# A gated convolution and pooling trunk: the input projection in pairs of blocks by seven partial products, its weight sums on GpSimd, its gates parked in DRAM

## The chip, the core and the metric

The kernel runs on one core of a Trainium2 chip. The metric is the device time of one execution in microseconds (us), here the median of several runs. A core has TensorE (PE, matrix products into the PSUM memory, whose weight loads are listed as PEld), VectorE (DVE), ScalarE (ACT), GpSimd (POOL) and SyncE (SP), which mostly issues DMAs. The engines run side by side, each through its own queue in a fixed order, and wait for one another by semaphores. SBUF is the on-chip memory that all engines and the DMAs reach.

## The reference

1024 prompt tokens with 16 meta tokens ahead of them, and 64 sample tokens (8 sequences of 8), pass one layer in float32; D is 1024.

```python
h = rmsnorm(x, norm_g)
z = einsum('btd,de->bte', h, w_in)          # w_in is 1024 x 7168
a_val, a_gate, a_silu, p_in, p_silu, g_a, g_b = split(z, 7)
u = a_val * sigmoid(a_gate)
c = causal_depthwise_conv(u, conv_w, conv_b) # width 31, per channel
c = silu(layernorm(c)) * silu(a_silu)
br_a = c @ w_conv_out
pooled = trailing_mean(p_in, 2/4/8/16 by channel group) - p_in
q = (pooled @ w_pool_mix, per group) * pool_scale * silu(p_silu)
br_b = q @ w_pool_out
y = x + (sigmoid(g_a) * br_a + sigmoid(g_b) * br_b) @ w_out
return rmsnorm(y, final_g), last 30 rows of u, last 15 rows of p_in
```

## The kernel before

Channels lie on the 128 partitions and tokens along the columns (1104 columns, 1088 without the meta tokens). Each matrix product is made of three float32r products: an operand is cut into a high part h (a rounded copy, ACT, `split` L98) and a low part l (the value minus h, DVE, L99), and `gemm` (L119 to L132, the matmul at L129) adds wh·xh + wh·xl + wl·xh in PSUM.

One block is 128 columns of w_in. It takes 8 slices of channels × 3 passes × 3 pieces of columns = 72 matmuls of 362 to 368 columns, each with its own weight load. w_in has 56 such blocks: convolution value and gate (`pv`, `pg` in `glu`), SiLU path (`psl`), pool input (`pp`), pool gate (`pps`), merge gates (`pga`, `pgb`). `load_w` fetches a block's 512 KB and splits it on ACT and DVE, three blocks ahead.

Order of the work: the first five `pp` blocks (NX = 5) multiply x·g before the RMS factor is known; the factor `rms` comes from `root_stats` and `spread`; then DVE scales x (L272) and it is split into hh and hl. Then come the pooling groups (`pool_in` with its window sums at L304 to L309, `pool_gates`, `pool_mix`). Then `ORDER` interleaves `glu`, `branch_b` (gate block `pgb` and projection `ppo`), `gate_a` and `silu_path`. A `glu` step ends with a convolution chunk (`conv_chunk`): 31 taps, one on ACT and 30 on DVE as scalar_tensor_tensor c = e·w + c (L378 for the prompt, L379 for the sample), put later in the order by CONV_LATER. Then LayerNorm (`pmean`, L462, `vsum`), `branch_a` (L475 to L477 and a split), the merge (`pco`, L500) and the output projection (`pwo`, L549). The engine queues' order comes from a list scheduler by program order and priority; two stretches at the start are fixed by hand.

GpSimd does little: memsets, and the copy of the sample's state into the extended tiles (L289, 120 columns; L404, 240 columns). SBUF work tiles come from 38 slots; PSUM has two tiles of three banks and two of one bank.

Of the kernel before, what the change touches and what calls it, by code (L numbers as in the profile page):

```python
# [10 lines left out]
ALU = mybir.AluOpType  # L11

P = 128
D = 1024
NK = D // P
META = 16
# [7 lines left out]
TP2 = SEQ  # L24
# [3 lines left out]
# Columns of a PSUM tile's three banks: of all tokens, and of all but the meta tokens. Counts are even.  # L28
CUT1 = (0, N1, 2 * N1, TALL)
CUT2 = (0, 364, 726, T2)  # L30
EW = CB + TP + DB * (CB + DS)
PW = TP + DB * (PB + DS)
# [3 lines left out]
NSLOT = 38  # L36
CONV_LATER = 4000
WARM = 8
NX = 5
# [10 lines left out]
def hybrid_trunk_kernel(  # L50
# [25 lines left out]
    wp = ctx.enter_context(tc.tile_pool(name="wp", bufs=3))  # L76
# [3 lines left out]
    ps3 = ctx.enter_context(tc.tile_pool(name="ps3", bufs=2, space=bass.MemoryType.PSUM))  # L80
    ps1 = ctx.enter_context(tc.tile_pool(name="ps1", bufs=2, space=bass.MemoryType.PSUM))

    def slot(name, n=T2, dt=F32):
        return sl.tile([P, n], dt, tag="slot", name=name, bufs=NSLOT, padded_shape=[P, TALL])

    def bank3(name):
        return ps3.tile([P, 3, 512], F32, tag="bank3", name=name)
# [9 lines left out]
    def split(dst_h, dst_l, src):  # L97
        act.copy(dst_h, src)  # L98
        dve.tensor_tensor(dst_l, src, dst_h.bitcast(F32), ALU.subtract)  # L99

    def load_w(src, name):
        raw = wp.tile([P, NK, P], F32, tag="raw", name=f"raw_{name}", bufs=2)
        h = wp.tile([P, NK, P], F32R, tag="wh", name=f"wh_{name}")
        l = wp.tile([P, NK, P], F32R, tag="wl", name=f"wl_{name}")
        sp.dma_start(out=raw, in_=src)

        def ready():
            split(h, l, raw)
# [13 lines left out]

    def gemm(out, w, xs, c0, cut, ns=range(3), nk=NK, m0=0, ks=None):
        wh, wl = w
        xh, xl = xs
        for k in ks or range(nk):
            for i, (a, b) in enumerate(((wh, xh), (wh, xl), (wl, xh))):
                for j in ns:
                    pe.matmul(  # L129
                        out[:, j, : cut[j + 1] - cut[j]],  # L130
                        a[:, k, m0 : m0 + P],
                        b[k][:, c0 + cut[j] : c0 + cut[j + 1]],  # L132
                        start=(k == 0 and i == 0),
                        stop=(k == nk - 1 and i == 2),
                    )
# [4 lines left out]
    # The pieces of a PSUM tile cut by CUT2, each with its columns of an SBUF tile.  # L140
    def pieces(ps, t):
        n, m = CUT2[1], CUT2[2] - CUT2[1]
        return (ps[:, 0, :n], t[:, :n]), (ps[:, 1:, :m], v3(t[:, n:], m))
# [9 lines left out]
    # 1 / sqrt(mean + eps) with tokens on partitions, a tile of tokens per pair of columns, from the  # L153
    # squares summed over chunks.
    def root_stats(ssum, n, eps, name):
        tiles = token_tiles(n)
        nt = len(tiles)
        ps = ps1.tile([P, 512], F32, tag="ps1", name=f"pst_{name}")
# [9 lines left out]
    # The factors of root_stats with tokens along the columns, on every partition.  # L168
    def spread(r, n, name):
        tiles = token_tiles(n)  # L170
        nt = len(tiles)
        out = slot(f"ir_{name}", n)
        for g in range(0, nt, 4):
            ps = ps1.tile([P, 512], F32, tag="ps1", name=f"pb_{name}{g}")
            part = tiles[g : g + 4]
            dg = slot(f"dg_{name}{g}", 4 * P)
# [12 lines left out]
    # The first NX blocks multiply x * g, and take the token's factor after the product.  # L189
    xs = [slot(f"x{k}", TALL) for k in range(NK)]  # L190
    xg = tuple([slot(f"xg{s}{k}", TALL, F32R) for k in range(NK)] for s in "hl")
# [13 lines left out]
    # Products that nothing reads bring the tensor engine to its full clock while the first loads run.  # L205
    warm = ps1.tile([P, 512], F32, tag="ps1", name="warm")
    for _ in range(WARM):
        pe.matmul(warm[:, :P], ones, ones, start=True, stop=True)
    xsum = slot("xsum", TALL)
    w_raw = [wp.tile([P, NK, P], F32, tag="raw", name=f"raw_p{i}", bufs=2) for i in range(2)]  # L210
    w_first = [tuple(wp.tile([P, NK, P], F32R, tag=f"w{s}", name=f"w{s}_p{i}") for s in "hl") for i in range(2)]
# [10 lines left out]
    load_w2 = load_w(w_in[PG + 2], "p2")  # L222
    out_first = [bank3(f"pp{j}") for j in range(2)]
    raws = []

    def keep_raw(j, ps):
        raw = slot(f"rawp{j}", TALL)
        act.copy(v3(raw, N1), ps[:, :, :N1])
        raws.append(raw)

    with tc.manual_schedule(engines={act.engine, dve.engine}):
# [8 lines left out]
        w = load_w2()  # L240
        for k in range(NK):
            for i in range(2):
                gemm(out_first[i], w_first[i], xg, 0, CUT1, ns=(0,), ks=(k,))
        for j in (1, 2):
            for i in range(2):
                gemm(out_first[i], w_first[i], xg, 0, CUT1, ns=(j,))
        act.activation(xsum, xs[0], AF.Square)
        for k in range(1, NK):
            sq = slot(f"xsq{k}", TALL)
# [7 lines left out]
    with tc.manual_schedule(engines={pe.engine}):  # L257
        for j in range(2, NX):
            if j > 2:
                w = load_w_now(w_in[PG + j], f"p{j}")  # L260
            out_raw[j] = bank3(f"pp{j}")
            for k in range(NK):
# [4 lines left out]
                gemm(out_raw[j], w, xg, 0, CUT1, ks=(k,))  # L267
            if j < NX - 1:
                keep_raw(j, out_raw[j])
    hx = ([], [])  # L270
    for k in range(NK):
        dve.scalar_tensor_tensor(xs[k], xs[k], col(OFF_NG, k), rms, ALU.mult, ALU.mult)  # L272
        h, l = slot(f"hh{k}", TALL, F32R), slot(f"hl{k}", TALL, F32R)
        split(h, l, xs[k])
        hx[0].append(h)
        hx[1].append(l)
    keep_raw(NX - 1, out_raw[NX - 1])

# [1 line left out]
    q = ([], [])  # L280
    st = ctx.enter_context(ExitStack())
    stp = st.enter_context(tc.tile_pool(name="stp", bufs=2))

    def pool_in(j, ps, pooled):
        e = stp.tile([P, PW], F32, tag="pe", name=f"pe{j}")
        es = e[:, TP:].rearrange("p (b t) -> p b t", t=PB + DS)
        stg = stp.tile([P, DB, PB], F32, tag="pst", name=f"pst{j}")
        sp.dma_start(out=stg, in_=spool[j])
        pool.tensor_copy(es[:, :, :PB], stg)  # L289
        if j < NX:  # L290
            dve.tensor_tensor(e[:, :TP], raws[j][:, :TP], rms[:, :TP], ALU.mult)
            dve.tensor_tensor(es[:, :, PB:], v3(raws[j][:, TP:], DS), v3(rms[:, TP:], DS), ALU.mult)
        else:
            act.copy(v3(e[:, : 2 * N1], N1), ps[:, :2, :N1])
            act.copy(e[:, 2 * N1 : TP], ps[:, 2, : TP - 2 * N1])
            act.copy(es[:, :, PB:], v3(ps[:, 2, TP - 2 * N1 : N1], DS))
# [369 lines left out]
```

## Time and profile before

| | us |
|---|---|
| median of 3 runs | 1015.0 (1014.75 to 1017.23) |
| span of the profiled execution | 1011.5 |
| PE busy | 1000.9 (99%), 5838 matmuls |
| DVE busy | 716.7 (71%) |
| ACT busy | 261.1 (26%) |
| POOL busy | 13.4 (1%) |

The span runs from the first to the last instruction of one profiled execution; a run's time has about 3.5 us around it (1015.0 less 1011.5). Rows of groups give the busy time of all instructions of a kind and the mean duration of one; pipelined instructions overlap, so busy time divided by the count is the spacing, and the mean is longer. Rows of the chain of waits give start, length and engine of each piece of the work that ended last. Rows of the timeline give start, duration, engine, line, operation and operands; x3 at the end of a row merges three.

### The profile page before, as it was taken

What the parts mean: (1) busy time and instruction counts of PE and PEld (TensorE: products, weight loads), DVE (VectorE), ACT (ScalarE), POOL (GpSimd) and SP (SyncE); (2) the same over time, 40 slices, a digit from 0 to 9 for tenths busy, and PEclk for the clock granted to TensorE, in tenths of its full rate; (3) what the DMA queues carried; (4) which work ended last, traced back from release to release, by engine and by line L of the source; (5) the groups of instructions that cost most, each with busy time, mean ns of one, the idle gap of its engine ahead of it and who ended that gap; (6) DMA issues with size and microseconds to landing.
All of it is one profiled execution on the core that took longest, in us unless ns stands there. A gap on an engine that the chain in (4) does not pass through costs nothing.

```text
span 1011.5 us, 13769 instructions
## 1 busy us (share of the span) xinstructions
PE 1000.9 (99%) x5838; PEld 978.2 (97%) x5838; DVE 716.7 (71%) x918; ACT 261.1 (26%) x344; POOL 13.4 (1%) x29
## 2 busy tenths in 40 slices
PE   8999999999999999999999999999999999999997
PEld 7999999999999999999999999999999999997885
DVE  6697753544999959769689799999846934445343
ACT  7644232222211111111121111111245722114111
POOL 0001100000000000000000000000000000000000
PEclk9999999999999999999999999999999999999999
DMA  8222222231212222221221232322111033334322
GB/s 276 68 38 63 61 49 49 45 68 39 48 65 52 90 51 83 69 48 64 70 48 64 68 93 49 101 45 90 64 42 43 23 149 131 130 131 174 124 77 84
DMA packets 45374, 79.02 MB, mean 78 GB/s; under 512 B 22912, under 2 KB 28032, under 8 KB 45312
## 3 DMA queue, kind: packets, MB, share of 16 engines
q1 hardware_dynamic: 43008, 69.22, 23.8%
q10 hardware_dynamic: 2304, 8.91, 2.6%
q8 instruction: 46, 0.75, 0.3%
q14 instruction: 16, 0.13, 0.0%
HBM read 63.09 MB, written 15.03 MB: 77 GB/s over the span
## 4 chain that ended last, share of the span: by engine, by line
PE 96%; DMA 1%; DVE 1%; SPq 0%; issue 0%; ACT 0%; DVEq 0%
PE pg L129 10%; PE pv L129 10%; PE psl L129 9%; PE ppo L129 9%; PE pps L129 9%; PE pga L129 9%; PE pgb L129 9%; PE pco L129 9%; PE pp L129 9%; PE pwo L549 7%; PE pmix L129 2%; DMA raw_wo<-in_w_out 1%; PE pwos L549 1%; DMA raw_p<-in_w_in 1%; DVE wol L99 0%
## 5 line engine op out<-in xcount | busy, mean ns | idle before, releaser
L378 DVE SCALAR_TENSOR_TENSOR c<-ce,pv,c 128x1024 f32<-128x1024 f32 x240 | 307.6, 1283 | 3.1
L379 DVE SCALAR_TENSOR_TENSOR c<-ce,pv,c 128x64 f32<-128x64 f32 x240 | 68.0, 283 | 5.6 <-ACT c L376 1.5
L500 DVE TENSOR_TENSOR lga<-pco,lga 128x364 f32<-128x364 f32 (+1 forms) x16 | 10.8, 719 | 46.8 <-PE pco L129 46.8
L129 PE MATMUL pg<-hh,wh_g 128*128 128x368 f32 x192 | 42.7, 330 | 0.0
L129 PE MATMUL pv<-hh,wh_v 128*128 128x368 f32 x192 | 42.6, 330 | 0.0
L129 PE MATMUL psl<-hh,wl_s 128*128 128x362 f32 (+1 forms) x192 | 42.6, 329 | 0.0
L129 PE MATMUL pg<-hl,wh_g 128*128 128x368 f32 x192 | 42.6, 330 | 0.0
L129 PE MATMUL psl<-hh,wh_s 128*128 128x362 f32 (+1 forms) x192 | 42.6, 329 | 0.0
L129 PE MATMUL pg<-hh,wl_g 128*128 128x368 f32 x192 | 42.6, 330 | 0.0
L129 PE MATMUL pv<-hh,wl_v 128*128 128x368 f32 x192 | 42.5, 330 | 0.0
L129 PE MATMUL pv<-hl,wh_v 128*128 128x368 f32 x192 | 42.5, 329 | 0.0
L129 PE MATMUL ppo<-ql,wh_po 128*128 128x362 f32 (+1 forms) x192 | 42.4, 329 | 0.0
L129 PE MATMUL pps<-hh,wl_ps 128*128 128x362 f32 (+1 forms) x192 | 42.4, 329 | 0.0
L129 PE MATMUL pga<-hh,wl_ga 128*128 128x362 f32 (+1 forms) x192 | 42.4, 329 | 0.0
L129 PE MATMUL pgb<-hh,wl_gb 128*128 128x362 f32 (+1 forms) x192 | 42.3, 328 | 0.0
L129 PE MATMUL ppo<-qh,wl_po 128*128 128x362 f32 (+1 forms) x192 | 42.3, 329 | 0.0
L129 PE MATMUL pco<-cxh,wh_co 128*128 128x362 f32 (+1 forms) x192 | 42.3, 328 | 0.0
L129 PE MATMUL pps<-hl,wh_ps 128*128 128x362 f32 (+1 forms) x192 | 42.2, 328 | 0.0
L129 PE MATMUL pgb<-hl,wh_gb 128*128 128x362 f32 (+1 forms) x192 | 42.2, 328 | 0.0
L129 PE MATMUL pga<-hl,wh_ga 128*128 128x362 f32 (+1 forms) x192 | 42.2, 328 | 0.0
L129 PE MATMUL psl<-hl,wh_s 128*128 128x362 f32 (+1 forms) x192 | 42.2, 328 | 0.0
L129 PE MATMUL pco<-cxl,wh_co 128*128 128x362 f32 (+1 forms) x192 | 42.2, 328 | 0.0
(212 smaller groups left out, 2210.9 us busy)
## 6 DMA issues: line engine op xcount, KB each, us to landing
x<-in_xT SPq DMA_DIRECT2D x24, 184.0 KB, 4.0
d_tb<-gbo ACTq DMA_DIRECT2D x8, 544.0 KB, 2.8
d_sga<-gao ACTq DMA_DIRECT2D x8, 544.0 KB, 3.4
t<-d_tb SPq DMA_DIRECT2D x8, 544.0 KB, 4.5
lga<-d_sga SPq DMA_DIRECT2D x8, 544.0 KB, 5.6
raw_ps<-in_w_in SPq DMA_DIRECT2D x8, 512.0 KB, 3.5
raw_g<-in_w_in SPq DMA_DIRECT2D x8, 512.0 KB, 4.2
raw_v<-in_w_in SPq DMA_DIRECT2D x8, 512.0 KB, 3.5
```

The costliest lines, as they stand in the source:

```text
L129: pe.matmul(out[:, j, : cut[j + 1] - cut[j]], a[:, k, m0 : m0 + P], b[k][:, c0 + cut[j] : c0 + cut[j + 1]], start=(k == 0 and i == 0), sto ...
L378: dve.scalar_tensor_tensor(cp, sp_, wk, cp, ALU.mult, ALU.add)
L379: dve.scalar_tensor_tensor(cs, ss_, wk, cs, ALU.mult, ALU.add)
L500: dve.tensor_tensor(c, p, c, ALU.mult)
L549: pe.matmul(ps[:, n - ns[0], :], x(k), w[k][:, n * 512 : (n + 1) * 512], start=(k == 0 and s == 0), stop=(k == NK - 1 and s == len(passes) ...
```

## The change

Four blocks (NX = 4) stay as they were. The other 52 blocks of w_in are made in 26 pairs by `seven`: a pair's weights are a 2×2 matrix of halves (two blocks × two halves of the 8 channel slices), the input is a 2×2 matrix too (two halves of the channel slices × two halves of the tokens, so the tokens are put in another order on the host), and seven products of half size with sums of their operands take the place of eight. Each product is 2 pieces of 276 (or 272) columns × 4 slices × 3 passes = 24 matmuls; a pair is 168.

- Input operands: seven sets of four tiles (`t_ops`, 28 of the now 37 slots), built once from the scaled x: 16 sums on DVE, 28 splits, of whose low parts 16 are on GpSimd and 12 on DVE.
- Weights, for each pair (`w_sums`): four sums and seven low parts on GpSimd, 11 tensor_tensor of 128×512; the high parts on ACT. Operand tiles: 6 (`wop`).
- Results: ACT copies three intermediate results of each pair out of PSUM (`keep`, 6 copies), DVE adds the others to them (`put`, 8 adds of 272 or 276 columns, PSUM + SBUF).
- PSUM is cut into 8 single banks, of which a pair uses all.
- Convolution: the prompt's taps stay on DVE; the sample's taps become products of 248 columns on GpSimd (8 for a chunk) and a tensor_reduce on DVE (2). `csum`, `vsum`, the sample's window sums and the low parts of pooled, mix weights and q go to GpSimd.
- All gates, the pooled inputs and the convolution results are written to DRAM and fetched again; `pool_mix`, `branch_b` and LayerNorm come after all 26 pairs.

```diff
-ORDER = "c0 b0 c1 b1 b2 c2 b3 b4 c3 b5 b6 c4 b7 a0 c5 a1 a2 c6 a3 a4 c7 a5 a6 a7 s0 s1 s2"
+ORDER = "g0 p2 p3 q0 g1 q1 q2 q3 b0 g2 b1 b2 b3 a0 g3 a1 a2 a3 s0 s1 s2 s3"
...
+    lo_, hi_ = slice(0, HT), slice(HT, TALL)
+    t_ops = {}
+    for name, k0 in (("11", 0), ("21", NQ)):
+        t_ops[name] = x_op(name)
+        for k in range(NQ):
+            x_split(t_ops[name][k], xs[k0 + k][:, lo_], pool if k % 2 else dve)
...
+    for k in range(NQ):
+        t = slot(f"ta{k}", (2, HT))
+        tmp.append(t)
+        dve.tensor_tensor(t[:, 0], xs[k][:, hi_], xs[k][:, lo_], ALU.subtract)
+        dve.tensor_tensor(t[:, 1], xs[NQ + k][:, hi_], t[:, 0], ALU.subtract)
+        x_split(t_ops["T2"][k], t[:, 1], pool if k % 2 else dve)
...
+    def w_sums(src, name):
+        a1, a2 = raw_tile(src[0], f"{name}0"), raw_tile(src[1], f"{name}1")
+        a11, a12, a21, a22 = a1[:, :NQ], a1[:, NQ:], a2[:, :NQ], a2[:, NQ:]
...
+        pool.tensor_tensor(s1, a21, a22, ALU.add)
+        pool.tensor_tensor(s2, s1, a11, ALU.subtract)
+        pool.tensor_tensor(s3, a11, a21, ALU.subtract)
+        pool.tensor_tensor(s4, a12, s2, ALU.subtract)
+        for i, a in enumerate((a11, a12, s2, s3, s1, s4, a22)):
+            o = op_tile(f"wo{i}_{name}", (2, NQ, P))
+            split(o[:, 0], o[:, 1], a, pool)
+            yield o
...
+        def keep(outs, what):
...
+                act.copy(c[:, :w], out[:, :w])
...
+        def put(block, half, outs, cs):
...
+                dve.tensor_tensor(z[block][:, half, cols[u]], out[:, :w], cs[u], ALU.add)
...
+        x = pair("px")
+        product(x, next(ws), t_ops["11"], units, True, False)
+        c1 = keep(x, "c1")
+        y = pair("py")
+        product(y, next(ws), t_ops["21"], units, True, True)
+        put(0, 0, y, c1)
+        product(x, next(ws), t_ops["T2"], units, False, False)
+        c2 = keep(x, "c2")
+        v = pair("pv")
+        product(v, next(ws), t_ops["T3"], units, True, False)
+        product(x, next(ws), t_ops["T1"], units, False, True)
+        c4 = keep(x, "c4")
+        put(1, 1, v, c4)
+        w = pair("pw")
+        product(w, next(ws), t_ops["22"], units, True, True)
+        put(0, 1, w, c4)
+        product(v, next(ws), t_ops["T4"], units, False, True)
+        put(1, 0, v, c2)
+        return z
...
+    def conv_chunk(i, e, es):
...
+                dve.scalar_tensor_tensor(cp, sp_, wk[:, k : k + 1], cp, ALU.mult, ALU.add)
...
+                pool.tensor_tensor(tap[:, b], win, wk.unsqueeze(1).to_broadcast([P, DS, CW]), ALU.mult)
+            dve.tensor_reduce(cs[:, h], tap.rearrange("p b t k -> p (b t) k"), AX.X, ALU.add)
...
+            pool.tensor_tensor(csum[0], csum[0], c, ALU.add)
+        act.dma_start(out=d_c[i], in_=c)
...
+            h, l = halves(fetch(d_pool[j], f"lp{j}"), f"pool{j}", pool)
...
+            h, l = halves(gate, f"q{j}", pool)
...
+            pool.tensor_tensor(vsum, vsum, sq, ALU.add)
```

## Rows read from the trace of the kernel before

**Rows 1.** The page: busy time of the engines, and the chain's shares by engine.

```profile
PE 1000.9 (99%) x5838; PEld 978.2 (97%) x5838; DVE 716.7 (71%) x918; ACT 261.1 (26%) x344; POOL 13.4 (1%) x29
PE 96%; DMA 1%; DVE 1%; SPq 0%; issue 0%; ACT 0%; DVEq 0%
```

**Rows 2.** Chain in order of time: start us, length us, what; whole blocks of the projection.

```profile
47.98 25.84 PE pp L129 x153
...
97.73 6.11 PE pmix L129 x36
103.85 23.91 PE pps L129 x144
...
229.78 12.10 PE pg L129 x72
241.89 12.07 PE pv L129 x72
...
959.51 44.58 PE pwo L549 x192
```

**Rows 3.** Groups of PE by form: operands, columns, count | busy us, mean ns.

```profile
L180 PE MATMUL pb_c<-dg_c,ones 128*128 128x128 f32 x18 | 2.3, 275 | 0.0
L160 PE MATMUL pst_x<-ones,xsum 128*128 128x2 f32 x18 | 2.1, 246 | 0.0
```

**Rows 4.** Timeline of GpSimd: its copies of 120 and 240 columns; start us, duration us.

```profile
25.82 0.52 POOL L289 COPY pe<-pst 128x120 f32<-128x120 f32 x2 [24.88 <-DMA pst<-in_spool]
81.86 1.30 POOL L289 COPY pe<-pst 128x120 f32<-128x120 f32 x1 [55.53 <-DVE pool L309]
...
139.97 0.29 POOL L289 COPY pe<-pst 128x120 f32<-128x120 f32 x1 [24.82 <-DVE pool L309]
...
302.03 0.39 POOL L404 COPY ce<-cst 128x240 f32<-128x240 f32 x1
...
632.63 2.39 POOL L404 COPY ce<-cst 128x240 f32<-128x240 f32 x1
```

**Rows 5.** Timeline of DVE around three of these copies (81.8, 302 and 632 us).

```profile
81.78 1.24 DVE L291 TENSOR_TENSOR pe<-rawp,ir_x 128x1040 f32<-128x1040 f32 x1
...
82.94 1.37 DVE L99 TENSOR_TENSOR pooll<-pool,poolh 128x1088 fp32r<-128x1088 f32 x1
...
302.09 0.93 DVE L405 TENSOR_TENSOR ce<-pv,sg 128x736 f32<-128x736 f32 x1
...
629.90 3.67 DVE L378 SCALAR_TENSOR_TENSOR c<-ce,pv,c 128x1024 f32<-128x1024 f32 x3
633.49 1.29 DVE L388 TENSOR_TENSOR csum<-csum,c 128x1088 f32<-128x1088 f32 x1
634.69 1.41 DVE L378 SCALAR_TENSOR_TENSOR c<-ce,pv,c 128x1024 f32<-128x1024 f32 x1
```

**Rows 6.** Groups of DVE by form: operands, columns, count | busy us, mean ns.

```profile
L378 DVE SCALAR_TENSOR_TENSOR c<-ce,pv,c 128x1024 f32<-128x1024 f32 x240 | 307.6, 1283 | 3.1
L99 DVE TENSOR_TENSOR cxl<-c,cxh 128x1088 fp32r<-128x1088 f32 x8 | 10.1, 1287 | 0.0
L308 DVE SCALAR_TENSOR_TENSOR pool<-pw,pe 128x1024 f32<-128x1024 f32 x8 | 9.8, 1219 | 0.1
L99 DVE TENSOR_TENSOR ml<-mraw,mh 128x512 fp32r<-128x512 f32 x4 | 2.7, 684 | 0.0
L406 DVE TENSOR_TENSOR ce<-pv,sg 128x304 f32<-128x304 f32 x8 | 3.7, 466 | 0.0
```

**Rows 7.** Groups of ACT by form: operands, columns, count | busy us, mean ns.

```profile
L98 ACT CAST mh<-mraw 128x512 fp32r<-128x512 f32 x4 | 2.5, 621 | 4.7 <-DMA mraw<-in_w_mix 4.6
L295 ACT COPY pe<-pp 128x304 f32<-128x304 f32 x3 | 1.2, 413 | 0.0
L467 ACT ACTIVATE csq<-c 128x1088 f32<-128x1088 f32 x7 | 7.8, 1115 | 4.5 <-DVE c L462 4.2
```

**Rows 8.** Timeline of DVE where the RMS factor is ready and x is scaled.

```profile
48.66 10.32 DVE L272 SCALAR_TENSOR_TENSOR x<-x,pv,ir_x 128x1104 f32<-128x1104 f32 x8 [2.58 <-ACT ir_x L185]
```

More of the change, by code (lines that the diff above doesn't have):

```diff
@@ new lines, in product @@
+    def product(outs, w, t, units, first, last):
+        for out, (lo, hi) in zip(outs, units):
+            for k in range(NQ):
+                for i, (a, b) in enumerate(((0, 0), (0, 1), (1, 0))):
+                    pe.matmul(
+                        out[:, : hi - lo],
+                        w[:, a, k],
+                        t[k][:, b, lo:hi],
+                        start=first and k == 0 and i == 0,
+                        stop=k == NQ - 1 and i == 2,
+                        skip_group_check=True,
+                    )
@@ new lines, in pool_window @@
+            pool.tensor_tensor(ss2[:, :, lo:], ss[:, :, lo:], ss[:, :, lo - d : PS - d], ALU.add)
+            s, ss, d = s2, ss2, 2 * d
+        dst = slot(f"pool{j}", (2, H2))
+        dve.scalar_tensor_tensor(
+            dst[:, :, :HP], v3(s[:, META:], HP), 1.0 / w, v3(e[:, META:], HP), ALU.mult, ALU.subtract
+        )
+        for h in range(2):
+            b = slice(h * DB // 2, (h + 1) * DB // 2)
+            dve.scalar_tensor_tensor(
+                v3(dst[:, h, HP:], DS), ss[:, b, PB:], 1.0 / w, es[:, b, PB:], ALU.mult, ALU.subtract
+            )
@@ new lines, in pool_window, with pool_ext, sample, pool_raw @@
+        act.dma_start(out=d_pool[j], in_=dst)
+    def pool_ext(j):
+        e = slot(f"pe{j}", (TP,))
+        es = st.tile([P, DB, PS], F32, tag="pes", name=f"pes{j}")
+        sp.dma_start(out=es[:, :, :PB], in_=spool[j])
+        return (e, es), (v3(e[:, :META], HM), v3(e[:, META:], HP), es[:, :, PB:])
+    def sample(z):
+        return z.rearrange("p h (b t) -> p (h b) t", t=DS)
+    def pool_raw(j):
+        e, (em, ep, es) = pool_ext(j)
+        f = parts(v3(rms, HT))
+        r = parts(v3(raws[j], HT))
+        dve.tensor_tensor(ep, r[1], f[1], ALU.mult)
+        pool.tensor_tensor(em, r[0], f[0], ALU.mult)
+        for h in range(2):
+            b = slice(h * DB // 2, (h + 1) * DB // 2)
+            pool.tensor_tensor(es[:, b], v3(r[2][:, h], DS), v3(f[2][:, h], DS), ALU.mult)
+        pool_window(j, *e)
@@ new lines, in pool_pair, with gate_pair @@
+    def pool_pair(i):
+        z = seven((w_in[PG + 2 * i], w_in[PG + 2 * i + 1]), f"p{i}", UNITS1, t_ops)
+        for b in range(2):
+            e, (em, ep, es) = pool_ext(2 * i + b)
+            zm, zp, zs = parts(z[b])
+            act.copy(em, zm)
+            act.copy(ep, zp)
+            for h in range(2):
+                act.copy(es[:, h * DB // 2 : (h + 1) * DB // 2], v3(zs[:, h], DS))
+            pool_window(2 * i + b, *e)
+    def gate_pair(i, base, name, func, dst):
+        z = seven((w_in[base + 2 * i], w_in[base + 2 * i + 1]), f"{name}{i}", UNITS2, t_ops)
+        for b in range(2):
+            act.activation(z[b], z[b], func)
+            act.dma_start(out=dst[2 * i + b], in_=z[b])
@@ new lines, in hybrid_trunk_kernel, with fetch @@
+    for j in range(NX):
+        with later():
+            pool_raw(j)
+    steps = {
+        "g": glu_pair,
+        "p": pool_pair,
+        "q": lambda i: gate_pair(i, PSG, "q", AF.Silu, d_gate),
+        "b": lambda i: gate_pair(i, GBG, "b", AF.Sigmoid, d_sgb),
+        "a": lambda i: gate_pair(i, GAG, "a", AF.Sigmoid, d_sga),
+        "s": lambda i: gate_pair(i, SG, "s", AF.Silu, d_sa),
+    }
+    for step in ORDER.split():
+        steps[step[0]](int(step[1]))
+    def fetch(src, name):
+        t = slot(name)
+        sp.dma_start(out=t, in_=src)
+        return t
@@ L467, in hybrid_trunk_kernel @@
             act.activation(sq, conv[i], AF.Square)
[L468 to L470 removed]
+            pool.tensor_tensor(vsum, vsum, sq, ALU.add)
+    for d in range(3, 6):
+        branch_b(d)
     rstd = spread(root_stats(vsum, T2, LN_EPS, "c"), T2, "c")
```

473 lines of the change are left out of this document (227 added, 246 removed).

## The prediction

> **What bounds the kernel now.** I read the page's busy times first, then the chain: PE is busy in 99% of the span and carries 96% of the chain [rows 1]. Then the chain in order of time: whole blocks of 72 matmuls follow one another without a gap [rows 2]. So a microsecond taken from PE is one off the time as long as every other engine keeps pace; DVE has 29% of the span free, ACT 74%, GpSimd 99%. Then what those engines would cost: GpSimd's few copies and what runs on DVE beside them [rows 4, 5], and DVE's and ACT's groups [rows 6, 7].
>
> **PE, the part that gains.** A block of 72 takes 12.10 us at 368 columns (168.0 ns a matmul), two of 362.7 take 23.91 us, and 192 matmuls of 512 columns take 44.58 us (232.2 ns) [rows 2]. From 368 to 512 columns that is 0.446 ns a column, so 276 columns come to 127.0 ns and 272 to 125.2 ns. A pair of 168 is 21.3 or 21.0 us. Of the 26 pairs 10 are made over all tokens (8 in the convolution, 2 of pool inputs) and 16 without meta tokens. Before: 10 × 24.17 + 16 × 23.91 = 624 us; after: 10 × 21.3 + 16 × 21.0 = 550 us. Gain 74 us. Could the loads, now 168 for 144, be the bound? Matmuls of 2 columns, which leave a load bare, are spaced by 2.1 / 18 = 117 ns, those of 128 columns (float32) by 128 ns [rows 3]. At 128 ns the stage is 559 us and the gain 65; I take 74.
>
> The Trainium skill (TensorE: Matmul & The Clock Gate, Back-to-back issue gap) gives N/2.4 + 2.5 ns for one matmul, an estimated 117.5 ns at 276 columns and a stage of some 509 us, a gain of 115. For 368 columns it would give 156 ns where the rows have 168.0, so the measurement decides.
>
> **GpSimd alone.** 11 tensor_tensor of 512 columns for each pair, 286 in all; no row of before has GpSimd doing one. Bounds: its copies take 0.26 to 0.29 us for 120 columns and 0.39 us for 240 where nothing stands in their way [rows 4], so 0.16 us and 0.96 ns a column. With both inputs read at once an op of 512 columns takes 0.65 us, with one after the other 1.14 us. I take 1.14: nearly twice DVE's 0.684 us for the same shape [rows 6], and I know no row that lets GpSimd read two streams at once. The Trainium skill (GPSIMD Engine Reference, Elementwise — side-by-side cycle accounting) has 4497 ns for 2048 columns, an estimated 1.12 us for 512; by it the sum would be the same. Of GpSimd's other work: 64 sample-tap products of 248 columns, 8 sums `csum` of 1088, 20 small window sums. All by the same price: 326 + 41 + 17 + 13 = 397 us in a stage of 550. It fits alone.
>
> **DVE alone.** 240 taps, spaced by (3.67 − 1.28) / 2 = 1.195 us [rows 5], stay: 287 us. 40 more with two SBUF inputs of 1024 to 1040 columns (20 window sums, 8 pool results, 4 scalings, 8 GLU products) at 1.14 us, from the 1219 ns of L308 less overlap [rows 6]: 45. 208 `put` of 272 to 276 columns at 0.44 us, below the 466 ns of 304 columns [rows 6]: 92. 16 reductions of 992 columns at 1.2 us: 19. Together 443 us. It fits alone. ACT has for a pair 7 copies of 0.62, 6 of about 0.39 and 2 activations of 1.1 us [rows 7], 9 of 21 us, and DMA stores; hidden, and so are the new DRAM writes and reads beside PE.
>
> **DVE and GpSimd together, the part that loses.** Rows 4 and 5 show that they don't run side by side. The copy at 81.86 takes 1.30 us in place of 0.27: it ends at 83.16, just behind the DVE op that began at 81.78 and ended at 83.02; the DVE op after that takes 1.37 us where its kind takes 1.29 [rows 5, 6]. Five of the eight copies of 120 columns look like this. The copy of 240 columns at 632.63 takes 2.39 us: it waits out a tap and `csum`, and the next tap takes 1.41 in place of 1.28 us. But at 302.03 the copy takes its 0.39 us beside a DVE op whose one input is in PSUM. So a DVE op with two SBUF inputs and a GpSimd op that reads SBUF take turns, and GpSimd's reading comes back as DVE time, less about 0.1 us: 240 columns are 0.23 us of reading and cost the tap 0.13. The Trainium skill (SBUF — State Buffer, Who interferes with whom) states it for each GpSimd instruction that reads SBUF, against each DVE one with two SBUF inputs: an exclusive lock for the whole instruction. The copies agree (1.30 for 0.27 us); a GpSimd op with two inputs is in no run here.
>
> So the two sums add up. GpSimd's turns: 0.98 us of reading less 0.1 = 0.88 us; 286 of them 252 us, sample taps 64 × 0.38 = 24, `csum` 15, the rest 7: 298 us. DVE's: 287 + 45 = 332 us. The input operands add 28 DVE ops of 552 columns at 0.64 and 16 GpSimd ops at 0.96: 33 us. Together 663 us of turns in a stage that PE could do in 550. Nor are they spread evenly: in about four pairs (the second of g0, before there is a convolution, and the last three, after it) DVE has few taps and the turns fill only 10.8 of 21 us, which leaves 41 us unused. The stage then takes 663 + 41 = 704 us, 154 more than PE needs. How this reaches PE: a pair's operands come from GpSimd, at most six ahead, so PE waits at the heads of the pairs, while the taps are finished at leisure.
>
> Bounds: at 0.65 us a GpSimd op (turn 0.39) the turns and gaps come to about 551 us and PE stays the bound; at 1.14 us with nothing overlapped and lost turns as at 632 us they come to 804.
>
> **Hand-overs.** *Start:* `rms` is ready at 48.66 us and the scaled x 10.3 us later [rows 8]; PE then has one direct block less to cover it. It does 153 matmuls from 47.98 [rows 2], of which the last 72 go, and so needs the first set at about 61.7. That set is ready by then; the later ones contend with GpSimd's 16 splits, inside the 663; without contention 3 us. *Mix:* 144 matmuls are 24 us of PE (6.11 us for 36 [rows 2]); GpSimd has 16 low parts of 1088 columns at 0.16 + 2.09 = 2.25 us and 4 of weights, 40.6 us, and a last chain of an ACT copy (1.1) and a low part, some 4 us: 40.6 − 24 + 4 = 21 us of PE waiting; at one stream 4, at worst 25. *LayerNorm:* branch_a has 8 × 3 DVE ops of 1.2 us [rows 6], 29 us, and behind the factor PE has two `ppo` blocks less some 8 us and the first `pco` block to cover it; with the weight splits in between 8 us, between 0 and 15.
>
> **Sum.** 1015 − 624 + 704 + 21 + 8 = 1124 us, made against the execution with a span of 1011.5 and about 3.5 us around it, which stands at the median. With the bounds: 1015 − 624 + 551 + 4 = 946 to 1015 − 624 + 804 + 40 = 1235.
>
> **Rivals.** *The forecast (slower):* taking turns holds the stage at some 704 us. For it: the copies, each time two SBUF inputs stood on DVE. It decides from a stage of 595 us (624 less 29 for the hand-overs) up, that is where GpSimd's turn for 512 columns is above 0.56 us, an op of some 0.82 us. *A, the turns cost little (faster):* GpSimd's reads slip between DVE's, or an op takes 0.65 us; PE stays the bound: 1015 − 74 + 3 + 21 + 8 = 973 us, 946 to 990. For it: each engine fits alone, and the order lets the convolution wait. Against it: rows 4 and 5. *B, the change doesn't do what it says:* loads hold 168 matmuls at 128 ns or above; 9 us more in A, nothing in the forecast, where PE waits anyway. Against it: 117 ns. *C, turns matter and the spare room covers half:* DVE's order puts many taps behind the last pairs and GpSimd runs free until then; the stage takes 600 us, 1020 us in all.
>
> **Chances.** Forecast 0.68, A and B together 0.22, C 0.10. Of C 0.06 go to slower, 0.03 to the same, 0.01 to faster. A measurement of this kernel can tell some 0.3% from no change. So slower 0.74, same 0.03, faster 0.23. The forecast's own range is 1030 to 1215. To hold 8 in 10 the range takes in C and half of A: 965 to 1215.
>
> **What would show it.** Right: GpSimd's tensor_tensor of 512 columns with means near 2 us in the stretches with taps and near 1.1 us without; taps with means well above 1283 ns; PE waiting for `wo` on GpSimd; a pair at 26 to 32 us in the middle and 21 to 22 us at the end; pairs' matmuls spaced by 125 to 128 ns when they run. Wrong: taps still at 1.28 us, PE above 95% through the pairs, or matmuls spaced by 140 ns or more. The prediction fails most easily by the price of GpSimd's op: each 0.1 us of it is 29 us.

## The result and the profile after

The changed kernel takes 1253.6 us (median of 4 runs, 1250.4 to 1254.7) beside 1016.1 us for the kernel before: a ratio of 1.234 (95% interval 1.232 to 1.236). Slower was right. The size was not: forecast were 109 us more, measured are 238, and the time lies above the range of 965 to 1215.

The span of the profiled execution is 1250.8 us. It splits as the sum of the prediction did (stage = from the first to the last matmul of the pairs):

| | forecast | measured | off by |
|---|---|---|---|
| first product of the pairs | 61.7 | 68.6 | +7 |
| the 26 pairs | 704 | 799.4 | +95 |
| mix stage, from its first matmul to the first `ppo` one | 45 (24 + 21) | 65.9 | +21 |
| what is left of the +64 us outside the pairs (29 forecast) | 8 | 15 | +7 |

The last row is the rest of a subtraction: outside the pairs the span has 1250.8 − 799.4 = 451.4 us, before 1011.5 − 624 = 387.5. Start and mix leave 64 − 7 − 42 = 15 us.

From the page after: busy times, the granted clock of PE in 40 slices, the chain, and the two groups that [rows 6] and the sample's taps answer to.

```profile
PE 999.1 (80%) x6462; PEld 962.2 (77%) x6462; DVE 864.4 (69%) x854; ACT 380.4 (30%) x637; POOL 758.1 (61%) x470
...
PEclk9876695787998889988799888999679998999999
...
PE 21%; DVE 1%; DMA 1%; ACT 0%; POOL 0%; issue 0%; POOLq 0%; SPq 0%; DVEq 0%; ACTq 0%
...
L475 DVE SCALAR_TENSOR_TENSOR c<-ce,pv,c 128x1024 f32<-128x1024 f32 x240 | 444.3, 1879 | 1.2
L483 POOL TENSOR_TENSOR tap<-ces,pv 128x248 f32<-128x248 f32 x64 | 71.2, 1145 | 0.2
```

PE was 99% busy in [rows 1] and is at 80%. No engine is full now. A tap has gone from 1283 to 1879 ns [rows 6]. The chain cannot be followed far back: its shares add up to about a quarter of the span, so the waits and the timeline have to tell the rest. PE's longest waits in the pairs:

```profile
PE py_p L339 <- DVE z_p L367: 38.5, 1, 38.5
PE pv_b L339 <- DVE z_b L367: 27.9, 4, 9.6
PE py_v L339 <- DVE z_g L367: 27.1, 1, 27.1
PE pv_a L339 <- DVE z_a L367: 26.8, 4, 10.6
PE pv_q L339 <- DVE z_q L367: 23.4, 3, 10.3
PE py_g L339 <- DVE z_q L367: 15.3, 1, 15.3
```

Each row names DVE's `z`, the result that `put` takes out of PSUM to free a bank. With the shorter ones they add up to 173 us in 19 waits. Waits for operands made on GpSimd (`tT`, `t`, `wo`) are 11 us. So PE waits for its results to be taken away, not for its operands as the prediction had it.

Two stretches of the timeline show the two ways. First a dense pair, at 426 to 447 us: DVE, GpSimd and PE.

```profile
426.17 15.24 DVE L475 SCALAR_TENSOR_TENSOR c<-ce,pv,c 128x1024 f32<-128x1024 f32 x7
441.34 0.78 DVE L367 TENSOR_TENSOR z_q<-pv_q,c_q 128x272 f32<-128x272 f32 x2
...
431.61 2.12 POOL L326 TENSOR_TENSOR s_g<-raw_g 128x512 f32<-128x512 f32 x1
433.69 2.24 POOL L110 TENSOR_TENSOR wo_b<-s_b,wo_b 128x512 fp32r<-128x512 f32 x1
436.00 2.12 POOL L327 TENSOR_TENSOR s_g<-s_g,raw_g 128x512 f32<-128x512 f32 x1
...
441.82 5.35 PE L339 MATMUL pv_q<-tT,wo_q 128*128 128x272 f32 x24 [10.27 <-DVE z_q L367]
447.01 3.19 PE L339 MATMUL px_b<-t,wo_b 128*128 128x272 f32 x24
```

Seven taps take 15.24 us, 2.18 each, and a GpSimd operation begins every 2.2 us: strictly one tap, one GpSimd operation, one tap. `put` stands behind the seven and PE waits 10.27 us. Behind that wait its 24 matmuls take 5.35 us, and the next 24 only 3.19: the granted clock has fallen in the pause, so part of the wait is paid a second time (the last section has its rows).

Then an early pair, at 178 to 232 us: DVE, GpSimd and PE again.

```profile
178.56 47.87 DVE L475 SCALAR_TENSOR_TENSOR c<-ce,pv,c 128x1024 f32<-128x1024 f32 x28
226.35 1.22 DVE L505 TENSOR_TENSOR ce<-z_v,z_g 128x1024 f32<-128x1024 f32 x1
227.48 0.79 DVE L367 TENSOR_TENSOR z_p<-py_p,c_p 128x276 f32<-128x276 f32 x2
...
226.50 2.02 POOL L488 COPY csum<-c 128x1088 f32<-128x1088 f32 x1 [22.28 <-DVE c L475]
...
227.98 1.06 PE L339 MATMUL py_p<-t,wo_p 128*128 128x276 f32 x3 [38.46 <-DVE z_p L367]
```

Here 28 taps of a whole convolution chunk stand in DVE's queue ahead of the `put`. GpSimd itself waits 22 us of it for the chunk, and PE waits 38.5 us. Most of this is the order of DVE's queue and not turn-taking: at 1.195 us a tap [rows 5] the 28 would still take 33.5 of the 47.9 us, and with taps that take no turns the same wait is still 24.6 us (first experiment).

### The profile page after: what moved, and what is told of

Read it like the earlier page. It is cut to its first block, busy times and chain, and to the rows that moved or that the text cites. A ratio compares the mean times of both kernels' runs of the same rounds, so it can differ in the third digit from the quotient of the medians.

```text
span 1250.8 us, 16084 instructions
## 1 busy us (share of the span) xinstructions
PE 999.1 (80%) x6462; PEld 962.2 (77%) x6462; DVE 864.4 (69%) x854; ACT 380.4 (30%) x637; POOL 758.1 (61%) x470
## 5 line engine op out<-in xcount | busy, mean ns | idle before, releaser
L475 DVE SCALAR_TENSOR_TENSOR c<-ce,pv,c 128x1024 f32<-128x1024 f32 x240 | 444.3, 1879 | 1.2
L483 POOL TENSOR_TENSOR tap<-ces,pv 128x248 f32<-128x248 f32 x64 | 71.2, 1145 | 0.2
L339 PE MATMUL pv_b<-tT,wo_b 128*128 128x272 f32 x192 | 32.5, 338 | 27.9 <-DVE z_b L367 27.9
L339 PE MATMUL pv_a<-tT,wo_a 128*128 128x272 f32 x192 | 32.6, 338 | 26.8 <-DVE z_a L367 26.8
L339 PE MATMUL pv_q<-tT,wo_q 128*128 128x272 f32 x192 | 32.7, 339 | 23.4 <-DVE z_q L367 23.4
L592 POOL TENSOR_TENSOR vsum<-vsum,csq 128x1088 f32<-128x1088 f32 x7 | 18.9, 2705 | 46.4 <-ACT csq L591 46.3
L339 PE MATMUL px_g<-tT,wo_g 128*128 128x276 f32 x192 | 32.5, 324 | 9.2 <-POOL tT L110 6.1
L339 PE MATMUL py_p<-t,wo_p 128*128 128x276 f32 x48 | 7.1, 302 | 38.5 <-DVE z_p L367 38.5
L110 POOL TENSOR_TENSOR wo_a<-s_a,wo_a 128x512 fp32r<-128x512 f32 x16 | 32.4, 2022 | 7.4 <-ACT wo_a L109 7.4
L110 POOL TENSOR_TENSOR wo_b<-s_b,wo_b 128x512 fp32r<-128x512 f32 x16 | 32.5, 2031 | 6.9 <-ACT wo_b L109 6.9
L110 POOL TENSOR_TENSOR wo_g<-s_g,wo_g 128x512 fp32r<-128x512 f32 x16 | 34.7, 2168 | 2.0 <-ACT wo_g L109 2.0
L339 PE MATMUL py_v<-t,wo_v 128*128 128x276 f32 x96 | 13.5, 295 | 27.1 <-DVE z_g L367 27.1
L110 POOL TENSOR_TENSOR wo_q<-s_q,wo_q 128x512 fp32r<-128x512 f32 x16 | 33.2, 2077 | 1.2 <-ACT wo_q L109 1.2
```

Source lines behind the costliest of these rows:

```text
L110: (low or dve).tensor_tensor(dst_l, src, dst_h.bitcast(F32), ALU.subtract)
L339: pe.matmul(out[:, : hi - lo], w[:, a, k], t[k][:, b, lo:hi], start=first and k == 0 and i == 0, stop=k == NQ - 1 and i == 2, skip_group_c ...
L475: dve.scalar_tensor_tensor(cp, sp_, wk[:, k : k + 1], cp, ALU.mult, ALU.add)
L483: pool.tensor_tensor(tap[:, b], win, wk.unsqueeze(1).to_broadcast([P, DS, CW]), ALU.mult)
L592: pool.tensor_tensor(vsum, vsum, sq, ALU.add)
```

## The experiments

Three theories of the stage's 799 us. TURNS: DVE operations with two SBUF inputs and GpSimd operations exclude one another, as forecast. QUEUE (ORDER in the first texts): DVE's queue has its order fixed ahead of time, and results stand in it behind taps, window sums and the building of the operand sets, whatever these read. SLOTS: the 28 slots of operand sets leave too little room, so that work is delayed until tiles come free. The kernel before took 1013.0 to 1013.7 us beside these runs. Each experiment is one execution; the changed kernel is the median of four. The mix stage is counted from its first matmul to the first `ppo` one. All of them:

| kernel | time | pairs | DVE, POOL busy in the pairs | mix |
|---|---|---|---|---|
| changed kernel | 1253.6 | 799.4 | 648, 671 | 65.9 |
| taps with one input | 1106.3 | 649.1 | 475, 499 | 66.8 |
| no taps | 1101.3 | 649.2 | 220, 496 | 66.2 |
| two operand sets | 1213.8 | 762.3 | 616, 653 | 65.7 |
| two sets, taps with one input | 1071.7 | 618.3 | 448, 478 | 66.1 |
| two sets, paced | 1181.2 | 722.8 | 644, 693 | 66.4 |
| two sets, paced, taps with one input | 1029.7 | 573.9 | 458, 473 | 65.7 |
| low parts of weights on DVE | 1221.1 | 772.4 | 671, 338 | 65.5 |
| all weight work on DVE | 1216.5 | 762.8 | 665, 184 | 64.5 |
| the same, two sets, paced | 1124.5 | 677.2 | 641, 183 | 65.3 |
| mix: low parts on DVE | 1241.5 | 797.7 | 650, 664 | 55.8 |
| the same, next pooled blocks early | 1235.8 | 799.6 | 649, 667 | 46.4 |

### Taps with one SBUF input

```diff
-                dve.scalar_tensor_tensor(cp, sp_, wk[:, k : k + 1], cp, ALU.mult, ALU.add)
+                two = sp_.rearrange("p h (t a) -> p h t a", a=2)
+                dve.tensor_reduce(cp[:, :, : HP // 2], two, AX.X, ALU.add)
```

> Each of the 30 convolution taps of a chunk is a tensor_reduce over pairs of the same 1024 elements: one SBUF input in place of two, about the same time on DVE (the kernel's 992-column reduction takes 1177 ns), the same places in DVE's queue. The convolution is not computed. Theory TURNS (a DVE op with two SBUF inputs and a GpSimd op that reads SBUF take turns; this stretches the taps to 2.2 us and, through DVE's queue, holds the results that PE waits for): the reductions are spaced by 1.2 us, GpSimd's 512-column ops fall from 1.7 to 2.2 us to about 1.3 us, PE's wait for DVE's results in the stage of pairs falls from 173 us to 30 to 50 us (a run of 29 taps still stands ahead of one result), the stage from 799 to about 620 us, the time to about 1075 us. Theory ORDER (the runs of taps ahead of the results in DVE's queue would hold PE at 1.2 us a tap just as well): the waits stay above 120 us and the time above 1190 us.

The time falls to 1106.3 us and the stage from 799.4 to 649.1. The stand-in takes as long as a tap alone, so it is the reading of two SBUF inputs that went, not DVE's time. (It also writes 512 columns where a tap writes 1024. No run takes this apart; in [rows 4, 5] a DVE operation that writes 736 columns and has one input in PSUM left the copy beside it at 0.39 us.) The groups of DVE and GpSimd in the pairs:

```profile
L476 DVE TENSOR_REDUCE c<-ce 128x512 f32<-128x1024 f32 x240 | 283.9, 1213 | 1.2
...
L110 POOL TENSOR_TENSOR wo_s<-raw_s,wo_s 128x512 fp32r<-128x512 f32 x12 | 15.4, 1291 | 13.1 <-ACT wo_s L109 13.1
```

Neither engine stretches the other now: 1213 ns a reduction, 1291 ns a GpSimd operation. Turns of the taps are worth 150 us of the stage. But the time is some 31 us above the expected one. The first two pairs are nearly as slow as in the changed kernel (97 us beside 99.5, with a wait of 25.3 us for `z`), and in the fourth a wait of 24.6 us for `z` is left.

### No taps at all

```diff
-                dve.scalar_tensor_tensor(cp, sp_, wk[:, k : k + 1], cp, ALU.mult, ALU.add)
+                pass
```

> The 30 DVE taps of each convolution chunk are left out (the convolution is not computed), so DVE has 444 us less to do as it was timed, and GpSimd's ops have almost no DVE op with two SBUF inputs beside them. Under TURNS and under ORDER PE comes near to being the bound of the stage: about 580 us, no low clock after its middle, a time of 1020 to 1040 us. If GpSimd were the bound by its own work (11 ops of 1.3 us for a pair and the sample's products, about 17 us of 21 for PE), the stage would stay above 650 us and the time above 1100 us.

1101.3 us, 61 above the expected range: a miss that tells more than a hit. The stage is 649.2 us, the same as with taps of one input, although DVE has 220 us of work instead of 475. So in sum a tap that takes no turns costs the stage nothing, though the losses aren't the same ones: the wait of 24.6 us behind the taps is gone, and PE waits 15 us for `c` on ACT, for which it does not wait with taps of one input. What is above PE's 550 us in both has another cause than the taps. GpSimd as the bound by its own work, the third case of the text above, is nearly met in its numbers (650 and 1100 us), but it isn't the cause: GpSimd is busy for 496 us of the 649, and further down a kernel with 473 us of GpSimd's work has a stage of 574.

### Two operand sets

```diff
-    for name in ("T2", "T3", "T1", "22", "T4"):
-        t_ops[name] = x_op(name)
...
-        x_split(t_ops["T4"][k], tmp3[k][:, 1], pool)
+    for name, of in (("T2", "11"), ("T3", "21"), ("T1", "11"), ("22", "21"), ("T4", "11")):
+        t_ops[name] = t_ops[of]
```

> Only two of the seven sets of input operands are built, and all seven products use these two; 20 of the 37 SBUF slots come free. The products are not those of the scheme; all matmuls, weight sums, taps and results stay. Theory SLOTS (the long waits of 38 and 27 us come from results that find no free slot, so that the queue was ordered with whole runs of taps ahead of them): both waits go, the stage falls from 799 to about 700 us and the time to about 1150 us. TURNS and ORDER: the waits stay nearly as they are; only the building of the operands at the start gets shorter, by 20 to 40 us, and the time is 1210 to 1235 us.

1213.8 us, the stage 762.3: 37 us less. PE's two waits in question, in this kernel:

```profile
PE py_p L319 <- DVE z_p L347: 38.5, 1, 38.5
PE py_v L319 <- DVE z_g L347: 11.8, 1, 11.8
```

With 20 slots free the pause of 38.5 us is as long as before, so SLOTS is out as its cause. The one of 27.1 us has shrunk to 11.8. In the changed kernel the window sums of the first pooled blocks stand in DVE's queue between the building of the sets and this result and begin at 109.9 us; here they begin at 71.2. That puts the gain down to the building, but this run frees the slots in the same edit and can't separate the two.

### Two sets and paced

The window sums, pooled blocks and convolution chunks become generators, and three DVE operations of them are released behind each `put`. The order of DVE's queue is then the program's: short pieces of taps between the results. The same edit takes the slots from 37 to 34 and the sample's buffers from two to four.

```diff
+PACE = 3
...
-                dve.tensor_tensor(z[block][:, half, cols[u]], out[:, :w], cs[u], ALU.add)
+                last = dve.tensor_tensor(z[block][:, half, cols[u]], out[:, :w], cs[u], ALU.add)
+            with tc.issue_after(last.ins):
+                pump(PACE)
...
-            with later():
-                conv_chunk(j, e, es)
+            pending.append(conv_chunk(j, e, es))
```

> Made from the kernel with two operand sets: DVE's queue gets at most a few taps between two results (three are released after each pair of results), no run of 29 any more. To be compared with that kernel. TURNS: the sum of the turns is the same, so the stage stays at 690 to 720 us as long as taps are spread over it, PE's waits become many short ones of 2 to 4 us and its clock stays up more; the time is 1130 to 1160 us. ORDER: without runs of taps ahead of the results PE waits little, the stage is about 600 us and the time about 1050 us.

1181.2 us, the stage 722.8 in place of 762.3, so the order is worth some 40 us beside the turns. It misses the expected 1130 to 1160. PE's waits for `z` are 97 us in 19 pieces, none above 13.5. DVE or GpSimd is busy in 711 of the 723 us.

### Two sets, paced, taps with one input

> The paced kernel with two operand sets, and in it each tap a reduction of pairs of columns of one SBUF input (so the convolution's values are left out, and five of the seven operand sets are copies by name of two others; the number of DVE instructions is that of the paced kernel). TURNS: the paced kernel's stage was 723 us with DVE or GpSimd busy in 714 of them; if that is the two engines taking turns, taps that need no turn leave the stage at what PE needs, 560 to 580 us, and the time at 1020 to 1040. QUEUE: if the paced kernel is still held by results standing behind DVE's work, whatever that work is, the stage stays above 660 and the time above 1115.

The edits of the last kernel and of the first together. 1029.7 us, stage 573.9, as TURNS has it. The stretches from the first to the last product of the pairs: start and end, length, then busy time and count of PE, PEld, DVE, ACT and POOL, the granted clock, DMA share, GB/s. First the changed kernel:

```profile
68.60:868.00 799.40, 602.52 (x4368) 592.23 (x4368) 647.95 (x547) 243.61 (x443) 671.17 (x427) 0.87 0.25 72
```

then the paced kernel with two sets:

```profile
71.40:794.20 722.80, 596.12 (x4368) 587.47 (x4368) 644.37 (x524) 230.76 (x423) 692.60 (x412) 0.92 0.25 79
```

and the same with taps of one input:

```profile
71.70:645.60 573.90, 556.76 (x4368) 554.42 (x4368) 458.41 (x524) 234.90 (x423) 473.44 (x412) 0.99 0.31 100
```

The last two have the same number of instructions on each engine; one form of tap is changed: 149 us. PE is at 97% of the stage and at 0.99 of its clock; from the eleventh pair on the pairs follow one another every 21.1 to 21.3 us, where 21.0 to 21.3 were worked out ahead. This is how the stage looks when nobody takes turns.

### Two sets, taps with one input, not paced

> The changed kernel with each tap a reduction of one SBUF input (the convolution's values are left out) and only two of the seven operand sets built (the other five are copies by name of those two); not paced. With the taps alone changed the stage was 649 us, with pacing and two sets as well 574. START: if the 75 us between them are the building of the sets, this kernel comes to 575 to 595 and 1030 to 1055 us in all. QUEUE: if they are the order of DVE's work, of which the window sums and taps ahead of results are a part whatever they read, it stays at 615 to 640 us, 1075 to 1100 in all.

1071.7 us, the stage 618.3, within what QUEUE named (its time 3 us below). Of the 75 us between 649 and 574 the sets are 31 and the order 44, with waits of 24.6 and 12.4 us for `z` in the first pairs. Where the taps do take turns, the same two steps are 37 (799 to 762) and 40 (762 to 723).

### Low parts of weights on DVE, and all weight work on DVE

```diff
-            split(o[:, 0], o[:, 1], a, pool)
+            split(o[:, 0], o[:, 1], a, dve)
```

and, in the second kernel only, the same change of engine for the four sums:

```diff
-        pool.tensor_tensor(s1, a21, a22, ALU.add)
+        dve.tensor_tensor(s1, a21, a22, ALU.add)
...
```

> The changed kernel with the seven low parts of each pair on DVE (about 0.68 us each) and the four sums left on GpSimd; nothing left out. TURNS: of the 286 GpSimd operations of 512 columns 182 go, with 1.18 us of turn each, and come back as 182 of 0.68 on DVE: 90 us less of turns, stage 799 to about 710, time about 1165 (1145 to 1190). QUEUE: if what counts is how much DVE work stands in the queue ahead of PE's results, 124 us more of it make the kernel slower: 1270 or more.

> The changed kernel with all eleven operations of each pair on DVE; GpSimd keeps the sample taps, sums and splits; nothing left out. TURNS: GpSimd's 337 us of turns go and 196 us of DVE work come; DVE alone needs about 660 us, so the stage is 670 to 710 us and the time 1125 to 1165, not above that of the kernel with only the low parts moved by more than 10 us; taps back at 1.25 to 1.30 us. QUEUE: 196 us more of DVE work ahead of results: 1290 or more.

1221.1 and 1216.5 us: both are faster, and both between what the two theories gave. In the second the turns are all but gone, and the stage is 763 us though DVE has only 665 us of work in it. The group of taps (page), then DVE and PE at 497 to 562 us (timeline):

```profile
L475 DVE SCALAR_TENSOR_TENSOR c<-ce,pv,c 128x1024 f32<-128x1024 f32 x240 | 310.1, 1322 | 0.8
```

```profile
498.11 59.87 DVE L475 SCALAR_TENSOR_TENSOR c<-ce,pv,c 128x1024 f32<-128x1024 f32 x50
557.90 0.78 DVE L367 TENSOR_TENSOR z_b<-py_b,c_b 128x272 f32<-128x272 f32 x2
...
558.38 3.99 PE L339 MATMUL py_b<-t,wo_b 128*128 128x272 f32 x16 [73.08 <-DVE z_b L367]
```

Fifty taps at 1.2 us each, hardly stretched, stand ahead of a `put` of 0.78 us, and PE waits 73 us. Four such pauses (73.1, 32.3, 20.5 and 16.2) are 142 us. So neither theory alone holds: each edit took turns away and QUEUE gave part of them back.

### All weight work on DVE, two sets, paced

> The paced kernel with two operand sets (five sets are copies by name of two others, so the convolution's and the gates' values differ), and in it all eleven operations of each pair on DVE. If the kernel with the weight work on DVE is slow by the order of DVE's queue alone, this one loses its long waits: DVE alone has some 645 us of work in the stage, so the stage is 650 to 680 us (763 without pacing and with all sets), the time 1100 to 1130, and PE waits for results in many short pieces. If instead GpSimd's remaining work (sample taps, sums) or the results themselves hold it, the stage stays above 710 and the time above 1160.

1124.5 us, stage 677.2, within the expected range of time and 86 us below the unpaced kernel (some 31 to 37 of them the sets). PE's longest waits in the pairs are now for operands:

```profile
PE pv_a L330 <- ACT wo_a L110: 9.7, 1, 9.7
PE pv_q L330 <- ACT wo_q L110: 7.7, 1, 7.7
PE pw_v L330 <- ACT wo_v L110: 7.1, 2, 5.0
```

Waits for `wo` are 75 us, for `z` 5. With turns and long pauses gone, DVE's own 641 us are above what PE needs. So moving the work off GpSimd trades turns for DVE's time; it is no way out either.

### The mix stage: low parts on DVE, then the next pooled blocks early

```diff
-            h, l = halves(fetch(d_pool[j], f"lp{j}"), f"pool{j}", pool)
+            h, l = halves(fetch(d_pool[j], f"lp{j}"), f"pool{j}")
...
-            h, l = halves(gate, f"q{j}", pool)
+            h, l = halves(gate, f"q{j}")
```

> The changed kernel with the 16 low parts of the mix stage and its 4 low parts of weights on DVE in place of GpSimd; nothing left out. GPSIMD HOLDS THE MIX STAGE: low parts of 1.3 us in place of 2.5 and none queued on GpSimd; the mix stage falls from 65 us to 40 to 45, the time by 20 to 25 us. THE FETCHES HOLD IT: PE's waits for the fetched pooled blocks and the gates (5 to 10 us for each of four groups) stay, and the stage is 60 us or more; the time moves by less than 6 us.

> The kernel with the mix stage's low parts on DVE (1241.5 us, mix stage about 56 us), and in it the fetch and the halves of a group's two pooled blocks written ahead of the gates of the group before; nothing left out. ORDER OF ACT'S QUEUE: the high parts of the next pooled blocks stood behind the high parts of this group's gated blocks; with them ahead PE's waits of 8.8, 10.1 and 7.1 us go, the mix stage is 32 to 40 us and the time 1218 to 1228. FETCHES: if the transfers through DRAM are late themselves, PE goes on waiting for the same blocks and the time moves by less than 5 us.

The second kernel also writes `ready = pooled_of(g + 1)` (fetch and halves) ahead of the gates of group g. The mix stage goes from 65.9 to 55.8 and then to 46.4 us, the time from 1253.6 to 1241.5 and 1235.8; the first lies between its two theories, the second took the waits mostly away but fell short of 32 to 40. Its time fell by 5.6 us only, since its first product comes 3 us later and its pairs take 2 us longer. PE and ACT in the changed kernel, in the mix stage (timeline):

```profile
904.28 1.28 PE L139 MATMUL pmix<-pool4h,m 128*128 128x364 f32 x3 [10.08 <-ACT pool4h L109]
908.29 1.27 PE L139 MATMUL pmix<-pool4l,m 128*128 128x364 f32 x3 [2.73 <-POOL pool4l L110]
...
902.13 1.10 ACT L109 CAST q3h<-lg 128x1088 fp32r<-128x1088 f32 x1 [3.93 <-DVE lg L558]
903.14 1.09 ACT L109 CAST pool4h<-lp 128x1088 fp32r<-128x1088 f32 x1
```

`pool4h` has its data long before (ACT waits for nothing ahead of it), but in ACT's queue it stands behind `q3h`, which waits for the gate product of the group before, which waits for PE. So the four groups run one after the other, each with a whole chain of PE, DVE, ACT and low part. With the order turned, PE's groups show:

```profile
L139 PE MATMUL pmix<-pool4h,m 128*128 128x362 f32 (+1 forms) x12 | 4.4, 430 | 1.5 <-ACT pool4h L109 1.5
...
L139 PE MATMUL pmix<-pool2h,m 128*128 128x362 f32 (+1 forms) x12 | 3.9, 382 | 3.3 <-ACT pool2h L109 3.3
...
L139 PE MATMUL pmix<-pool6h,m 128*128 128x362 f32 (+1 forms) x12 | 3.7, 367 | 3.1 <-ACT pool6h L109 3.1
```

10.1 us has become 1.5. What is left here is short waits and matmuls at 367 to 430 ns instead of about 330, with the granted clock at 0.82 over this mix stage and at 0.63 in its third quarter.

## Why the prediction was right in sign and wrong in size

The stage, from what PE needs to what it took, each step one difference between two kernels:

| | stage | step |
|---|---|---|
| PE at 21.0 to 21.3 us a pair, as forecast | 550 | |
| two sets, paced, no turns of taps | 574 | +24 first pairs and low clock |
| not paced | 618 | +44 order of DVE's queue |
| all seven sets built | 649 | +31 building of sets (the slots that they take included) |
| taps with two SBUF inputs | 799 | +150 turns |

The steps depend a little on the order in which they are taken: turns are 144 to 150 us, the order 40 to 44, the sets 31 to 37.

**Turn-taking: right in mechanism, a turn priced too low.** The prediction had 154 us of stage above PE's 550, and 33 us of turns for the operand sets are in them. The taps' turns are 150 us as the difference of 799 and 649, 149 between the two paced kernels, 144 between the two with two sets and no pacing. So 150 beside 154 looks like a hit, but that is partly luck: the building of the sets comes on top with 31, which makes 181 where 154 were forecast. The 27 us between them fit the price: GpSimd's operation is dearer (1.29 us alone where 1.14 was taken), and the turn is 0.98 us, not 0.88: seven taps in 15.24 us are 2.18 each, 0.98 above the 1.195 of [rows 5]. For 286 operations 0.1 us more of turn is an estimated 29 us. The Trainium skill (SBUF — State Buffer, Who interferes with whom) has the exclusive lock between a GpSimd operation that reads SBUF and a DVE operation with two SBUF inputs; the trace agrees, with 2.18 us a tap where the engines meet and 1213 ns for a DVE operation of one input beside the same GpSimd work.

**The step that failed: "PE waits at the heads of the pairs, while the taps are finished at leisure".** The sum counted turns as work that fills the stage without loss and took it that PE would see them only through late operands. PE's rows after say `z`: 173 us of waits behind DVE's queue, 11 us behind GpSimd's operands. Taps aren't finished at leisure; they stand ahead of the results that free PSUM, and a pair uses all eight banks. A row of before showed that DVE's order is fixed in runs: three taps in one row of [rows 5]. What no row showed is how long such a run becomes when the result behind it is due. That is +44 us here, and with the work moved to DVE much more (one pause of 73 us). Of the 95 us by which the stage missed its 704, this order is 44, the price of the turns 27, and the first pairs and the low clock behind pauses 24. Why the list scheduler put whole chunks ahead of due results, no run shows.

**"Inside the 663": the sets' size was right, their place wrong.** They were counted with 33 us among the turns and cost 31. But the sum let them cost time only as a part of turns that fill the stage, and they cost it even where the taps take none, since PE has nothing else to do while they are built: the first seven products take 48.6 us, and with two sets 28.4. The first product is 7 us late as well. DVE around the RMS factor in the changed kernel:

```profile
38.12 4.52 DVE L261 TENSOR_TENSOR xsum<-xsum,xsq 128x1104 f32<-128x1104 f32 x2
...
53.87 9.26 DVE L290 SCALAR_TENSOR_TENSOR x<-x,pv,ir_x 128x1104 f32<-128x1104 f32 x6 [4.77 <-ACT ir_x L193]
```

and in the kernel with all weight work on DVE:

```profile
39.68 1.30 DVE L261 TENSOR_TENSOR xsum<-xsum,xsq 128x1104 f32<-128x1104 f32 x1
...
49.16 10.78 DVE L290 SCALAR_TENSOR_TENSOR x<-x,pv,ir_x 128x1104 f32<-128x1104 f32 x8 [2.59 <-ACT ir_x L193]
```

The sums of squares, 1.30 us each there, take 4.52 for two beside GpSimd's first weight operations: x is scaled from 53.87 us on where it was 48.66 [rows 8]. With the weight work on DVE the first product is at 63.9 us instead of 68.6.

**PE's gain: right where it runs, not over the stage.** Pairs that nothing holds follow every 21.1 or 21.3 us, as forecast from [rows 2]. But PE is busy for 602 us of the stage, not 550: its mean granted clock there is 0.87 of full speed in the changed kernel and 0.99 in the paced kernel whose taps take no turns, where it is busy for 557. None of the sum's terms had the clock behind a pause.

**Mix stage: mis-sized, 45 where it takes 66 us.** GpSimd's low parts were costed at 2.25 us and take 2.5; they hold 10 us, by the first experiment there. Another 9 were in ACT's queue, an order that the prediction didn't look at. The pairs end just inside their bound of 804 us; that the time lies above even the bound of 1235 comes from this stage (42 us above the 24 of its products, where 25 was the worst) and from the start (7 us, none was put). LayerNorm and merge cost 15 us where 8 were forecast, by subtraction; no run took this apart.

**DVE and ACT: right.** The taps with one input leave DVE 475 us in the stage, where 443 and 28 operations of the sets (18) were forecast; `put` takes 427 to 446 ns (0.44 forecast). ACT is busy for 244 us of the stage, and 9 us a pair make 234.

**Rivals.** A and C are out: turns cost what was forecast, and more. B is out: 21.1 and 21.3 us a pair are 126 and 127 ns a matmul, below its 128. (The turn at which the forecast begins to hold comes out as 0.53 us, not 0.56, on a straight line between the prediction's own 551 and 704 us; nothing hangs on it.) The missing rival was one that ended above the forecast, with the same turns and a queue that loses time besides.

**Could it be mended?** With turns and order gone, and two sets only, the kernel is at 1029.7 us, above before's 1013.7, though its pairs take 574 us where 624 were needed: start, mix and the rest give 66 us back. The shorter mix stage would take some 20 off, an estimate from 65.9 and 46.4 us, and bring it level; but with real taps and real sets 150 + 31 come on again. Pacing with all seven sets wasn't tried: the paced kernel has 34 slots with 8 of them for its two sets, and seven take 28. So no version here beats the kernel before, and none that computes the layer comes within 200 us of it.

## What to carry to other kernels

Where an engine's queue takes results out of PSUM, ask not only whether its work fits into the stage but what stands ahead of each result: a run of whole chunks there stops PE even while the engine has time left over the stage. Count work on GpSimd as DVE's wherever DVE reads two SBUF inputs, and test that by a stand-in with one input and the same duration; here it moved the stage by 150 us. A move from one engine to another is judged by the sum of both and by the order that results from it, not by the share of idle time that the receiving engine shows.

## What the runs showed of the hardware

- DVE and GpSimd alternate operation by operation: a tap of 1.2 us alone comes every 2.18 us, and a GpSimd operation of 1.29 us alone takes 2.12 to 2.28. By these numbers GpSimd's operation keeps an estimated 0.3 us of its time outside the exclusion (1.29 alone, 0.98 of turn). The sums of 552 columns that build the sets show the same: 0.72 us alone, 1.8 to 1.9 beside GpSimd's splits.
- A DVE reduction of one SBUF input (1213 ns, one every 1.18 us) isn't held up by steady GpSimd work, nor is `put`, with one input in PSUM: its mean is 434 ns in the changed kernel and 438 ns where all weight work is on DVE.
- GpSimd's tensor_tensor with nobody in its way: 1.29 us for 512 columns, 680 to 700 ns for 248, 2.5 us for 1088. The Trainium skill (GPSIMD Engine Reference, Elementwise — side-by-side cycle accounting) has 4497 ns for 2048 columns, an estimated 1.12 us for 512, which is 0.17 below what was measured.
- A wait on PE costs time behind it, too. Stretches of the changed kernel around the pause at 432 us, in the same columns as above:

```profile
425.00:431.50 6.50, 6.50 (x53) 6.32 (x51) 6.50 (x5) 1.92 (x4) 6.50 (x3) 1.00 0.41 126
431.50:441.80 10.30, 0.04 (x1) 0.00 (x0) 10.30 (x7) 0.62 (x1) 10.07 (x6) 0.73 0.05 22
441.80:447.00 5.20, 5.18 (x24) 5.18 (x25) 5.20 (x8) 1.11 (x1) 0.74 (x1) 0.55 0.02 3
447.00:452.00 5.00, 5.00 (x42) 5.00 (x41) 5.00 (x5) 2.91 (x5) 3.96 (x3) 1.00 0.54 223
```

  PE is busy before it at 1.00 of its clock (2.4 GHz), idle for 10 us in which the granted clock falls, busy again at 0.55 (mostly the level of 1.2 GHz), then back at 1.00. That is 5.35 us for 24 matmuls in place of 3.19. Over the stage PE's busy time came to 602 us where 550 were worked out.
